# A seventh pair of row tiles in seven block products, with the last pair's sums in the place of x^T

## The chip, the cores and the metric

The kernel runs on one core of one Trainium2 chip. The metric is the device time of one execution in microseconds; three executions of the kernel before were timed, and one more was profiled. Engines are named as in the profile: PE (TensorE, matrix products), DVE (VectorE), ACT (ScalarE), POOL (GpSimd), SP (SyncE, which issues the loads).

## The reference

Two layers of an encoder over 256 tokens of width 1024, each a half-step feed-forward, a mixer of two groups of attention heads, and another half-step feed-forward, every one followed by a layer norm. The change touches the feed-forward blocks, of which there are four:

```python
def swiglu(x, w_in, w_out):
    h = x @ w_in
    gate, up = h[..., :D_FF], h[..., D_FF:]
    return (jax.nn.silu(gate) * up) @ w_out
...
    x = layer_norm(ALPHA * x + 0.5 * swiglu(x, ffn1_w_in[l], ffn1_w_out[l]), ln_g[l, 0], ln_b[l, 0])
```

With `D_FF` = 2816, the hidden activation g has 22 column tiles of 128, and `w_out` has 22 row tiles of 128 x 1024. The product g @ `w_out` is called the second product here, x @ `w_in` the first.

## The kernel before

All products are made in fp32 precision from two fp32r halves: a value is split into a high half (`wh` of a weight, made by a copy on ACT) and a low half (`wl`, made on DVE as value minus high half, L73 and L119), and each product is the sum of three matmuls: high by high, high by low, low by high. All weights are loaded from memory once, as row tiles of 128 x 1024 (512 KB), into five buffers named `raw`; the halves have nine buffers each.

A feed-forward block goes as follows. The first four column tiles (`first`) and then the other 18 (`col`, in twos) of g are computed transposed, so that g has its columns on the partitions: for each column tile 16 wide matmuls of 512 columns (L419) with x^T, high and low half side by side in the tile `xx`, and 16 narrow ones of 256 columns (L424). `xx` holds x^T as 8 blocks of (half, token tile, 128). DVE and ACT then apply SiLU, multiply and split g.

Then comes the second product, whose result has four blocks: two tiles of 128 tokens by two halves of 512 columns. There are two ways to add a row tile of `w_out` to it. A *single* (`step`, L503) takes 12 matmuls of 512 columns for one row tile: 3 parts, 2 token tiles, 2 halves. A *pair* (`pair`, L527) takes two row tiles together as a 2 x 2 block product in seven products instead of eight (Winograd's form of Strassen's scheme): 21 matmuls for two row tiles. Four of the seven products gather in PSUM tiles `pp` over all pairs and are combined at the end (L540 to L549); three go straight to the accumulators `acc`. For a pair, `_make_pair` (L76 and on) loads both row tiles (`a` and `b`) and makes four combinations of their blocks on DVE (L86 to L89: into `t`, into a half of `a`, and into `t4`, whose halves are the tiles ending in `f`), and then the halves of `b`, `t`, `a` and `f` (L73; three tiles of 1024 columns and one of 512). On the other side, `sums` (L448 on) makes four combinations of the pair's blocks of g: four steps of 128 columns on DVE into `sf`, a copy of 512 on ACT (L461) for the high halves, and a difference of 512 on DVE (L462) for the low ones. The sums stay until their pair is used. Those of the first three pairs lie in buffers of `xp`, beside the residual x; those of the next three lie in the pool `tp` (tag `tmp`, seven buffers, two for each pair).

The order on PE is written out by hand. `STR` names the pairs of row tiles that go as pairs. The other row tiles are singles; the last seven of them are the *tail*, and `PLAN` gives the order of the rest: `o` is a single and `S` a pair. After the plan the tail runs over the first token tile, then over the second, while the first one's layer norm runs. In before, pairs 3 to 8 (row tiles 6 to 17) are pairs, row tiles 0, 1, 2 are the singles of the plan, and 3, 4, 5, 18 to 21 are the tail. The other engines' orders come from a scheduler, which follows the program's order and priorities; preparing a weight has a low priority, and `W.get` asks for weights up to nine half-buffers ahead (a pair counts as four).

The weights of the first block's plan and tail are numbered 44 on: in before the singles are 44, 45 and 47, the pairs 46 and 48 to 52, the tail 53 to 59; so `wl52a` is the low half of the last pair's `a`.

Of the kernel before, what the change touches and what calls it, by code (L numbers as in the profile page):

```python
# [24 lines left out]
JT = DFF // P  # L25
# [12 lines left out]
NB = 4  # L38
LATER = 100
WARM = 9  # L40
STR = (3, 4, 5, 6, 7, 8)
PLAN = "o o S o S S S S S"

# [90 lines left out]
def encoder_kernel(  # L136
# [36 lines left out]

    singles = [k for k in range(JT) if k // 2 not in STR]
    singles, tail = singles[: len(singles) - TAIL], singles[len(singles) - TAIL :]
    plan, left, pairs = [], list(singles), list(STR)
    for u in PLAN.split():
        plan.append((u, (left if u == "o" else pairs).pop(0)))
# [28 lines left out]
    xx = cp.tile([P, KT, 2, 2, P], F32R, name="xx")  # L207
# [153 lines left out]
    def ffn(l, n, last=False):  # L361
# [42 lines left out]
        def col(*js, flip=False):  # L404
# [26 lines left out]
            for j, hs, tl, ws in ts:  # L431
                for s in range(2):
                    two(hs, ws, s)
                    nc.scalar.copy(tl[:, s], hs[s][:, 1, :])  # L434
                    dv.tensor_tensor(tl[:, s], hs[s][:, 0, :], tl[:, s], ALU.add)  # L435
                nc.scalar.activation(tl[:, 0], tl[:, 0], AF.Silu)  # L436
                gv = tl[:, 1]
                dv.tensor_tensor(gv, tl[:, 0], gv, ALU.mult)  # L438
                q, jj = divmod(j, 2)
                n = P if q in STR and jj == 0 else SEQ  # L440
                nc.scalar.copy(gs[q][:, jj, 0, 0:n], gv[:, 0:n])  # L441
                dv.tensor_tensor(gs[q][:, jj, 1, 0:n], gv[:, 0:n], gs[q][:, jj, 0, 0:n].bitcast(F32), ALU.subtract)
                if q in STR and jj:
                    sums(q, ts[0][2][:, 1], gv)
# [3 lines left out]
        def sums(q, g0, g1):  # L448

            f = tp.tile([P, 4, P], F32, tag="tmp", name=f"sf_{nm}_{q}")  # L450
            if STR.index(q) < 3:
                s = xp.tile([P, 2, 4, P], F32R, tag="x", name=f"s_{nm}_{q}")
                sh, sl = s[:, 0], s[:, 1]
            else:
                sh, sl = (tp.tile([P, 4, P], F32R, tag="tmp", name=f"s{c}_{nm}_{q}") for c in "hl")
            a11, a21, a12, a22 = g0[:, 0:P], g0[:, P:SEQ], g1[:, 0:P], g1[:, P:SEQ]
            dv.tensor_tensor(f[:, 0], a21, a22, ALU.subtract)
            dv.tensor_tensor(f[:, 1], a11, f[:, 0], ALU.subtract)
            dv.tensor_tensor(f[:, 2], a21, a11, ALU.subtract)
            dv.tensor_tensor(f[:, 3], a12, f[:, 1], ALU.subtract)  # L460
            nc.scalar.copy(sh, f)  # L461
            dv.tensor_tensor(sl, f, sh.bitcast(F32), ALU.subtract)  # L462
            sm[q] = sh, sl
# [43 lines left out]
        def pair(q, w, first, final):  # L507
            b11, b21, b22, t4, t1, t2, t3 = w
            if first:
                for c in (5, 7, 1, 6):  # L510
                    pp[c] = ps.tile([P, 512], F32, tag="b", name=f"pp_{nm}_{c}")
            sh, sl = sm[q]
            blk = lambda kk, t: [gs[q][:, kk, e, t * P : (t + 1) * P] for e in range(2)]
            smb = lambda c: (sh[:, c], sl[:, c])
            s1, s2, s3, s4 = (smb(c) for c in range(4))
            for o, (ah, al), (bh, bl) in (
                (acc[0][0][1], blk(1, 0), b21),
                (acc[0][1][1], s4, b22),
                (pp[5], s1, t1),
                (pp[7], s3, t3),  # L520
                (pp[1], blk(0, 0), b11),
                (pp[6], s2, t2),
                (acc[1][0][1], blk(1, 1), t4),
            ):
                own = any(o is p for p in pp.values())
                for e, (g, ww) in enumerate(((ah, bh), (ah, bl), (al, bh))):
                    mm(o, g, ww, start=(own and first and e == 0), stop=(own and final and e == 2))  # L527

        for u, k in plan:
            w = W.get(wi)  # L530
            wi += 1
            if u == "S":
                pair(k, w, k == STR[0], k == STR[-1])
            else:
# [3 lines left out]
        c = 0.5 / ALPHA  # L538
# [24 lines left out]
        for n_, (i, cs) in enumerate(todo):  # L563
# [3 lines left out]
            if last and cs is acc[1] and i == TAIL - SPLIT - 1:  # L567
                s, a = acc[1][1][:2]
# [413 lines left out]
```

## Time and profile before

| | |
|---|---|
| three timed runs | 928.75, 930.30, 930.32 us; median 930.3 |
| the profiled execution | 929.28 us, span 927.5 us |
| granted PE clock, mean | 0.997 |
| PE busy | 99% of the span |
| DVE busy | 87% |
| ACT busy | 62% |
| read from memory | 174.35 MB, 189 GB/s over the span |

The second product with its tail takes some 57 us in each of the four blocks; in the first block it begins at 128 us of the span. In the timeline view a row gives the start in us, the duration in us, the engine, the line, the operation with the tiles written and read, and in brackets the idle time just before with what ended it. Instructions of one engine overlap a little in their pipelines, so what an engine can do is read from start to start, not from the durations.

### The profile page before, as it was taken

To read this page: it belongs to the slowest core of one execution; us is meant where nothing else is said; L and a number is where in the kernel's file an instruction comes from. 1 tells how busy PE (TensorE), PEld (TensorE's weight loads), DVE (VectorE), ACT (ScalarE), POOL (GpSimd) and SP (SyncE) were. 2 spreads that over 40 slices of the span, in tenths; PEclk is the share of its full clock that TensorE was granted. 3 is DMA by queue.
4 is the path that set the end of the run, shared out by engine and by line. 5 is a ranking of instruction groups with operands and counts; after the bars stand their busy time and mean duration, and the time that the engine had idled before them with its cause. 6 is when DMAs were issued, how large, how long until landed. Compare 5 with 4: busy or idle time off the path is not lost.

```text
span 927.5 us, 13795 instructions
## 1 busy us (share of the span) xinstructions
PE 919.1 (99%) x4958; PEld 784.9 (85%) x4958; DVE 804.9 (87%) x1388; ACT 577.8 (62%) x982; POOL 17.0 (2%) x27
## 2 busy tenths in 40 slices
PE   9999999999999999999999999999999999999996
PEld 6888888888878888888888888888888888888885
DVE  7898899998987677899986888999988876888997
ACT  5768656546865666656646666664478656666660
POOL 0000000000000000000000000000000000000000
PEclk9999999999999999999999999999999999999998
DMA  8976445774426755545775665466844365665451
GB/s 320 313 265 203 160 137 191 246 260 154 128 90 206 248 182 182 159 136 191 257 262 196 187 192 168 136 231 208 290 112 137 100 236 188 189 192 163 136 205 46
DMA packets 51380, 176.30 MB, mean 190 GB/s; under 512 B 6512, under 2 KB 8304, under 8 KB 51312
## 3 DMA queue, kind: packets, MB, share of 16 engines
q1 hardware_dynamic: 51024, 175.03, 58.0%
q8 instruction: 39, 0.64, 0.3%
q10 hardware_dynamic: 288, 0.39, 0.1%
q14 instruction: 29, 0.24, 0.1%
HBM read 174.35 MB, written 1.05 MB: 189 GB/s over the span
## 4 chain that ended last, share of the span: by engine, by line
PE 98%; DMA 1%; DVE 1%; SPq 0%; issue 0%; ACT 0%; DVEq 0%
PE hg L419 14%; PE hu L419 14%; PE acc L503 12%; PE hb L381 9%; PE hu L424 7%; PE hg L424 7%; PE pp L527 7%; PE acc L527 5%; PE ao L840 5%; PE os L776 1%; PE pj_sq L617 1%; PE pj_sq L619 1%; PE pj_dv L617 1%; PE pj_sq L618 1%; PE pj_dq L618 1%; PE pj_dv L619 1%
## 5 line engine op out<-in xcount | busy, mean ns | idle before, releaser
L119 DVE TENSOR_TENSOR wl<-raw,wh 128x1024 fp32r<-128x1024 f32 (+1 forms) x271 | 325.2, 1207 | 57.0 <-PE hg L424 20.2
L118 ACT CAST wh<-raw 128x1024 fp32r<-128x1024 f32 (+1 forms) x271 | 282.1, 1046 | 99.7 <-PE acc L503 14.8
L419 PE MATMUL hg<-xx,wh 128*128 128x512 f32 x576 | 143.1, 390 | 0.0
L419 PE MATMUL hu<-xx,wh 128*128 128x512 f32 x576 | 142.3, 389 | 0.0
L419 PEld LDWEIGHTS hu<-xx,wh 128*128 128x128 f32 x576 | 108.1, 188 | 22.5
L419 PEld LDWEIGHTS hg<-xx,wh 128*128 128x128 f32 x576 | 106.6, 188 | 21.2
L503 PE MATMUL acc<-wh,g 128*128 128x512 f32 (+1 forms) x326 | 90.5, 386 | 0.0
L424 PE MATMUL hg<-xx,wl 128*128 128x256 f32 x576 | 81.0, 283 | 0.0
L424 PE MATMUL hu<-xx,wl 128*128 128x256 f32 x576 | 80.9, 283 | 0.0
L424 PEld LDWEIGHTS hg<-xx,wl 128*128 128x128 f32 x576 | 75.4, 191 | 1.6
L424 PEld LDWEIGHTS hu<-xx,wl 128*128 128x128 f32 x576 | 74.3, 192 | 0.0
L503 PEld LDWEIGHTS acc<-wh,g 128*128 128x128 f32 x326 | 60.9, 188 | 12.2
L381 PE MATMUL hb<-wh,xx 128*128 128x512 f32 x256 | 69.5, 391 | 0.4 <-ACT wh L118 0.4
L381 PEld LDWEIGHTS hb<-wh,xx 128*128 128x128 f32 x256 | 47.7, 188 | 11.3 <-ACT wh L118 1.6
L503 PE MATMUL acc<-wl,g 128*128 128x512 f32 (+1 forms) x163 | 51.7, 385 | 0.0
L434 ACT COPY tl<-hg 128x256 f32<-128x256 f32 x72 | 26.7, 371 | 30.9 <-PE hg L419 27.4
L434 ACT COPY tl<-hu 128x256 f32<-128x256 f32 x72 | 26.9, 373 | 19.6 <-PE hu L424 16.8
L381 PE MATMUL hb<-wl,xx 128*128 128x512 f32 x128 | 38.9, 390 | 0.0
L441 ACT CAST g<-tl 128x128 fp32r<-128x128 f32 (+1 forms) x72 | 26.7, 371 | 19.2 <-DVE tl L438 18.2
L840 PE MATMUL ao<-wh,xx 128*128 128x512 f32 x128 | 37.0, 398 | 0.0
L503 PEld LDWEIGHTS acc<-wl,g 128*128 128x128 f32 x163 | 30.6, 188 | 6.1
L436 ACT ACTIVATE tl<-tl 128x256 f32<-128x256 f32 x72 | 30.1, 418 | 6.5 <-DVE tl L435 5.7
(1140 smaller groups left out, 1576.3 us busy)
## 6 DMA issues: line engine op xcount, KB each, us to landing
raw<-in_f_in_dram SPq DMA_DIRECT2D x144, 512.0 KB, 4.4
raw<-in_f_out_dram SPq DMA_DIRECT2D x40, 512.0 KB, 4.5
raw<-in_m_in_dram SPq DMA_DIRECT2D x36, 512.0 KB, 4.4
raw<-in_f_b_dram SPq DMA_DIRECT2D x29, 512.0 KB, 4.3
raw<-in_m_out_dram SPq DMA_DIRECT2D x8, 512.0 KB, 5.0
raw<-in_m_out_dram SPq DMA_DIRECT2D x16, 256.0 KB, 4.4
lng<-in_ln_g_dram SPq DMA_DIRECT2D x6, 512.0 KB, 4.9
lnb<-in_ln_b_dram SPq DMA_DIRECT2D x6, 512.0 KB, 6.2
```

Of the source, the lines that this page charges most:

```text
L118: nc.scalar.copy(wh[:, s], raw[:, s])
L119: nc.vector.tensor_tensor(wl[:, s], raw[:, s], wh[:, s].bitcast(F32), ALU.subtract)
L381: mm(hb[s], xx[:, k, g, t, :], ww[:, 512 * s : 512 * s + 512], start=(k == 0 and e == 0), stop=(k == KT - 1 and e == 2))
L419: mm(hs[s], ws[s][0][:, k * P : (k + 1) * P], xx[:, k], start=(k == 0 and not flip), stop=(k == KT - 1 and flip), skip_group_check=flip)
L424: mm(hs[s][:, 1, :], ws[s][1][:, k * P : (k + 1) * P], xx[:, k, 0], start=(k == 0 and flip), stop=(k == KT - 1 and not flip), skip_group_c ...
L434: nc.scalar.copy(tl[:, s], hs[s][:, 1, :])
L436: nc.scalar.activation(tl[:, 0], tl[:, 0], AF.Silu)
L441: nc.scalar.copy(gs[q][:, jj, 0, 0:n], gv[:, 0:n])
L503: mm(a, g, ww[:, s], start=(k == ka and e == 0), stop=(k == kb and e == 2))
L527: mm(o, g, ww, start=(own and first and e == 0), stop=(own and final and e == 2))
L617: mm(o, xx[:, k, 0, t, :], wh[:, s], start=(k == 0), stop=False)
L840: mm(acc[t][h], xx[:, k, g, t, :], ww[:, s], start=(k == 0 and e == 0), stop=(k == KT - 1 and e == 2))
```

## The change

Pairs 4 to 10 go as pairs, seven in place of six; row tiles 0 to 7 are the singles, 0 in the plan and 1 to 7 in the tail. The plan is one single and then seven pairs in a row. The last pair's sums of g (tiles 20 and 21) get no buffers of their own: their high and low halves are written over the first two blocks of `xx`, x^T, which has been read by then.

```diff
-STR = (3, 4, 5, 6, 7, 8)
-PLAN = "o o S o S S S S S"
+STR = (4, 5, 6, 7, 8, 9, 10)
+PLAN = "o S S S S S S S"
...
             if STR.index(q) < 3:
                 s = xp.tile([P, 2, 4, P], F32R, tag="x", name=f"s_{nm}_{q}")
+                sh, sl = s[:, 0], s[:, 1]
+            elif q == JT // 2 - 1:
+                s = xx[:, 0:2].rearrange("p k e t c -> p k (e t) c")
                 sh, sl = s[:, 0], s[:, 1]
             else:
                 sh, sl = (tp.tile([P, 4, P], F32R, tag="tmp", name=f"s{c}_{nm}_{q}") for c in "hl")
```

Lines after L453 stand three further down in the changed kernel (L457 to L462 are L460 to L465 there, L540 to L549 are L543 to L552). The first block's single of the plan is weight 44, the pairs are 45 to 51, the tail 52 to 58.

The scheduler's order on DVE moves with it, in the same way in all four blocks. The first place is the end of the first products in the first block, behind the last step on column tile 21 (`tl_21`); `sf_10` are the sums of tiles 20 and 21. Before:

```order
L438 TENSOR_TENSOR tl_21_1376<-tl_21_1376 128x256
L73 TENSOR_TENSOR wl48t<-raw48t,wh48t 128x1024
L442 TENSOR_TENSOR g_10_198<-tl_21_1376,g_10_198 128x256
L87 TENSOR_TENSOR raw49t<-raw49a,raw49b 128x512
L73 TENSOR_TENSOR wl48a<-raw48a,wh48a 128x1024
L88 TENSOR_TENSOR raw49a<-raw49b,raw49t 128x512
L73 TENSOR_TENSOR wl48f<-t_48_1496,wh48f 128x512
L89 TENSOR_TENSOR t_49_1547<-raw49b,raw49a 128x512
L73 TENSOR_TENSOR wl49b<-raw49b,wh49b 128x1024
```

And now:

```order
L438 TENSOR_TENSOR tl_21_1370<-tl_21_1370 128x256
L86 TENSOR_TENSOR raw47t<-raw47a 128x512
L442 TENSOR_TENSOR g_10_198<-tl_21_1370,g_10_198 128x256
L460 TENSOR_TENSOR sf_10_1451<-tl_20_1341,tl_21_1370 128x128
L87 TENSOR_TENSOR raw47t<-raw47a,raw47b 128x512
L461 TENSOR_TENSOR sf_10_1451<-tl_20_1341,sf_10_1451 128x128
L88 TENSOR_TENSOR raw47a<-raw47b,raw47t 128x512
L463 TENSOR_TENSOR sf_10_1451<-tl_21_1370,sf_10_1451 128x128
L465 TENSOR_TENSOR xx<-sf_10_1451,xx 128x512
L89 TENSOR_TENSOR t_46_1467<-raw46b,raw46a 128x512
L73 TENSOR_TENSOR wl46f<-t_46_1467,wh46f 128x512
L89 TENSOR_TENSOR t_47_1530<-raw47b,raw47a 128x512
```

At this place DVE now makes the last pair's sums between the combinations of pair 47's weights, writes their low halves into `xx`, and only then makes `t4` of pair 46 and its low half; before, no sums stood here.

The second place is the end of the plan in the first block, from the last pair's `a` on: `wl_` with a number is a low half of a tail weight, `x_in` the residual, `v` and `u` the tiles in which the block products are combined. Before:

```order
L73 TENSOR_TENSOR wl52a<-raw52a,wh52a 128x1024
L73 TENSOR_TENSOR wl52f<-t_52_1700,wh52f 128x512
L119 TENSOR_TENSOR wl_1723<-raw_1721,wh_1722 128x1024
L119 TENSOR_TENSOR wl_1750<-raw_1748,wh_1749 128x1024
L119 TENSOR_TENSOR wl_1756<-raw_1754,wh_1755 128x1024
L119 TENSOR_TENSOR wl_1762<-raw_1760,wh_1761 128x1024
L540 SCALAR_TENSOR_TENSOR x_in_601<-pp_1_1519,x_in_601 128x512
L543 TENSOR_TENSOR v_1793<-pp_6_1520,v_1793 128x512
L119 TENSOR_TENSOR wl_1768<-raw_1766,wh_1767 128x1024
L545 TENSOR_TENSOR u_1797<-pp_5_1517,v_1793 128x512
L119 TENSOR_TENSOR wl_1806<-raw_1804,wh_1805 128x1024
L540 SCALAR_TENSOR_TENSOR x_in_601<-u_1797,x_in_601 128x512
```

And now:

```order
L73 TENSOR_TENSOR wl51a<-raw51a,wh51a 128x1024
L73 TENSOR_TENSOR wl51f<-t_51_1718,wh51f 128x512
L119 TENSOR_TENSOR wl_1741<-raw_1739,wh_1740 128x1024
L119 TENSOR_TENSOR wl_1768<-raw_1766,wh_1767 128x1024
L543 SCALAR_TENSOR_TENSOR x_in_593<-pp_1_1502,x_in_593 128x512
L546 TENSOR_TENSOR v_1811<-pp_6_1503,v_1811 128x512
L119 TENSOR_TENSOR wl_1774<-raw_1772,wh_1773 128x1024
L548 TENSOR_TENSOR u_1815<-pp_5_1500,v_1811 128x512
L119 TENSOR_TENSOR wl_1780<-raw_1778,wh_1779 128x1024
L543 SCALAR_TENSOR_TENSOR x_in_593<-u_1815,x_in_593 128x512
L550 TENSOR_TENSOR v_1811<-pp_7_1501,v_1811 128x512
L119 TENSOR_TENSOR wl_1786<-raw_1784,wh_1785 128x1024
```

Four tail weights stood ahead of the first step of the combination, and now two; the seventh tail weight now has seven steps of the combination ahead of it, where it had five.

## Prediction

> **What bounds the kernel now.** I read the page first, then the waits of PE (TensorE), then DVE (VectorE) and PE in order of time through the second products of the first feed-forward block.
>
> ```profile
> span 927.5 us, 13795 instructions
> PE 919.1 (99%) x4958; PEld 784.9 (85%) x4958; DVE 804.9 (87%) x1388; ACT 577.8 (62%) x982; POOL 17.0 (2%) x27
> PEclk9999999999999999999999999999999999999998
> ```
>
> ```profile
> PE wps L217 <- PEq L971: 0.8, 1, 0.8
> PE hb L381 <- ACT wh L118: 0.4, 1, 0.4
> ```
>
> PE is busy for 919.1 of 927.5 us at the full granted clock, and the two waits shown, 1.2 us together, are all that the waits view has for it, both in the first 11 us. So every matmul that goes is worth its time, and every wait that comes is paid in full. The next engine is DVE, and in the stretch that the change touches it is hardly behind. In this row of the windows view (length, busy us of PE, weight loads, DVE, ACT and POOL, then clock, DMA share and GB/s):
>
> ```profile
> 128.00:165.00 37.00, 37.00 (x165) 30.65 (x164) 36.06 (x44) 23.91 (x29) 0.00 (x0) 1.00 0.56 186
> ```
>
> DVE works 36.06 of 37 us. It makes the weights' low halves (`wl`) and the pairs' four combinations. One pair of the steady run, on DVE in order of time (start, duration), and the last `a` tile of the last pair:
>
> ```profile
> 146.97 0.69 DVE L86 TENSOR_TENSOR raw51t<-raw51a 128x512 f32<-128x512 f32 x1
> 147.57 0.69 DVE L87 TENSOR_TENSOR raw51t<-raw51a,raw51b 128x512 f32<-128x512 f32 x1
> 148.18 1.22 DVE L73 TENSOR_TENSOR wl51b<-raw51b,wh51b 128x1024 fp32r<-128x1024 f32 x1
> 149.31 0.68 DVE L88 TENSOR_TENSOR raw51a<-raw51b,raw51t 128x512 f32<-128x512 f32 x1
> 149.91 1.22 DVE L73 TENSOR_TENSOR wl51t<-raw51t,wh51t 128x1024 fp32r<-128x1024 f32 x1
> 151.05 0.68 DVE L89 TENSOR_TENSOR t<-raw51b,raw51a 128x512 f32<-128x512 f32 x1
> 151.65 1.22 DVE L73 TENSOR_TENSOR wl51a<-raw51a,wh51a 128x1024 fp32r<-128x1024 f32 x1
> 152.79 0.68 DVE L73 TENSOR_TENSOR wl51f<-t,wh51f 128x512 fp32r<-128x512 f32 x1
> 153.39 0.68 DVE L86 TENSOR_TENSOR raw52t<-raw52a 128x512 f32<-128x512 f32 x1
> ...
> 158.07 1.22 DVE L73 TENSOR_TENSOR wl52a<-raw52a,wh52a 128x1024 fp32r<-128x1024 f32 x1
> ```
>
> From 146.97 to 153.39 a pair takes DVE 6.42 us with no gap: five steps of 512 columns that follow each other by 0.60 and three of 1024 by 1.135 (5 x 0.60 + 3 x 1.135 = 6.41). PE over the last pair (first matmul; the first that reads `wl52a`; then the tail, with the first and the seventh `wl`):
>
> ```profile
> 160.04 0.39 PE L527 MATMUL acc<-wh52b,g 128*128 128x512 f32 x1
> ...
> 162.99 0.39 PE L527 MATMUL pp<-wl52a,g 128*128 128x512 f32 x1
> ...
> 164.80 0.61 PE L503 MATMUL acc<-wh,g 128*128 128x512 f32 x2
> 165.25 0.62 PE L503 MATMUL acc<-wl,g 128*128 128x512 f32 x2
> ...
> 173.41 0.62 PE L503 MATMUL acc<-wl,g 128*128 128x512 f32 x2
> ```
>
> 160.04 to 164.80 is 4.76 us for 21 matmuls, 0.2267 us each. So PE eats a pair in 4.76 us and DVE makes one in 6.41: within a run of pairs PE gains 1.65 us per pair on DVE. It gets away with it today because DVE starts early: `wl52a` is ready at 158.07 + 1.22 = 159.29 and read at 162.99, a slack of 3.70 us. The other blocks stand the same:
>
> ```profile
> L73 DVE TENSOR_TENSOR wl138a<-raw138a,wh138a x1: 1212/1212/1212, 436.3 to 436.3; 128x1024 fp32r<-128x1024 f32 x1
> L527 PE MATMUL pp<-wl138a,g x1: 389/389/389, 441.2 to 441.2; 128*128 128x512 f32 x1
> L73 DVE TENSOR_TENSOR wl284a<-raw284a,wh284a x1: 1217/1217/1217, 894.3 to 894.3; 128x1024 fp32r<-128x1024 f32 x1
> L527 PE MATMUL pp<-wl284a,g x1: 389/389/389, 899.2 to 899.2; 128*128 128x512 f32 x1
> ```
>
> Here too 4.9 us lie between the two starts, as in the first block (158.07 and 162.99).
>
> **The change part by part.** *Removed on PE.* Two row tiles as singles cost 24 matmuls, as a pair 21: three fewer in each of four blocks, 12 x 0.2267 = 2.72 us. That is all there is to gain.
>
> *Added on DVE ahead of the last pair.* The rows of other kinds that the count needs (steps of 128, then of 256; the brackets give DVE's idle time and its releaser):
>
> ```profile
> 97.07 0.29 DVE L459 TENSOR_TENSOR sf<-tl 128x128 f32<-128x128 f32 x1
> 97.27 0.28 DVE L457 TENSOR_TENSOR sf<-tl,tl 128x128 f32<-128x128 f32 x1
> 97.48 1.22 DVE L119 TENSOR_TENSOR wl<-raw,wh 128x1024 fp32r<-128x1024 f32 x1
> ...
> 101.26 0.69 DVE L462 TENSOR_TENSOR sl<-sf,sh 128x512 fp32r<-128x512 f32 x1 [0.69 <-ACT sh L461]
> ...
> 113.12 0.69 DVE L462 TENSOR_TENSOR sl<-sf,sh 128x512 fp32r<-128x512 f32 x1 [1.13 <-ACT sh L461]
> ...
> 118.06 0.41 DVE L435 TENSOR_TENSOR tl<-hu,tl 128x256 f32<-128x256 f32 x1
> 118.39 0.41 DVE L442 TENSOR_TENSOR g<-tl,g 128x256 fp32r<-128x256 f32 x1
> ```
>
> Small steps follow by 0.20 (128 columns) and 0.33 (256). I count in DVE's order from `sl` of the pair of tiles 16 and 17 (113.12) to the start of the last pair's `a`. Before: 19 steps of 1024, 26 of 512, 16 of 256 = 42.5 us (158.07 - 113.72 = 44.35 measured, so 1.8 us of it is waiting). After: 20, 33, 14, and 10 of 128 (two pairs' sums, which before were made earlier in the block) = 49.2 us. That is 6.67 us more (1.135 + 7 x 0.60 - 2 x 0.335 + 10 x 0.20). The start of the stretch stays put, because DVE waits there in both: the rows at 101.26 and 113.12 show it waiting for ACT's copy of the sums, behind work that PE releases.
>
> *Extra waits.* Ahead of the last `a`, DVE now waits for ACT's copy of the new sums (0.69, the row at 101.26) and then takes `wl46f` directly behind the step that makes its input, so it waits for ACT again (0.7, by the same kind of copy). At most 1.4, at least 0 if the 1.8 us of waiting shrink by as much; I take 0.7, the middle, since only part of that waiting is of this kind. Queued behind both waits on DVE is every later pair; PE waits for those.
>
> *When PE wants it.* Two singles fewer (2 x 2.72) and one pair more (4.76) ahead of it: 0.68 earlier, at 162.31. DVE has it at 159.29 + 6.67 + 0.7 = 166.66. PE thus waits **4.35 us** over the run of pairs (3.65 to 5.05). It begins at the fifth pair: taken back by 1.65 per pair from 4.35, the waits have added up to 2.70 at the sixth and 1.05 at the fifth, and the fourth still lies 0.6 ahead of PE.
>
> *The tail.* The seven tail weights were made ahead of the tail, with the block products' combination put in between. The seventh in before:
>
> ```profile
> 170.99 1.21 DVE L119 TENSOR_TENSOR wl<-raw,wh 128x1024 fp32r<-128x1024 f32 x1
> ```
>
> 170.99 + 1.21 = 172.20, read at 173.41: 1.2 us of slack. After, from the last `a` to the seventh tail `wl`, DVE has 8 steps of 1024 and 8 of 512 up to the end of it (12.75 us between the two starts, by 1.135 + 0.60 + 6 x 1.135 + 7 x 0.60), and PE 8 matmuls, six tail tiles at 1.36 and 0.45: 10.42. Coming from a pair that PE waited for, it waits **2.33 us** more. A wait for a transfer can add to this, as one did in before:
>
> ```profile
> 167.56 1.05 ACT L118 CAST wh<-raw 128x1024 fp32r<-128x1024 f32 x1 [2.36 <-DMA raw<-in_f_out_dram]
> ```
>
> In before the stretch took 12.92 instead of the counted 11.54, so 2.33 to 3.7; I take 2.4, the low end, because DVE runs later against the loads than it did.
>
> *What follows.* The other half of the tail (9.5 us of PE) needs no new weight; the layer norm has one step of 512 less and one of 1024 more ahead of it, 0.5 us, against a start that is 0.5 us earlier behind the accumulators' end. I cost it at nothing; were that cover gone, it costs 0.5 per block. What DVE owes is paid by PE's waiting, so the next stage starts with the old lead.
>
> *The sums in the place of x^T.* They are made from the last column tiles' results, so the matmuls that read x^T last are done before there is anything to write: no wait. The transposed rows return there only after the tail's first half, which stands behind the last pair on PE. *ACT* gets the high halves of the same tiles to copy and is busy 23.91 of 37. *DMA*: the same bytes, two loads of a pair for two single ones on SP's queue, which the added pair moves past nothing else; in the steady run above DVE never waited for a load. POOL has nothing. All these at nothing; if a pair's load were late by its whole slack, it would show as a DVE wait for ACT or DMA, at most the 2.36 us of the row above.
>
> *Restart of PE* after a wait, bounded by the length of a weight load that may have to come first (the 188 ns of this group):
>
> ```profile
> L503 PEld LDWEIGHTS acc<-wh,g 128*128 128x128 f32 x326 | 60.9, 188 | 12.2
> ```
>
> 0 to 0.19, 0.1 taken.
>
> **Sum per block**: 4.35 + 2.4 + 0.1 - 0.68 = 6.2 us, four times 24.7. The profiled run took 929.28 (span 927.5 and 1.8 around it): 954.0. The median of the three runs, 930.3, lies 1.0 above it, so I forecast **955.0 us**.
>
> [...]
>
> **Rivals.**
> *The lead holds (faster).* If DVE still had every pair ahead of PE, only the 12 matmuls would count: 930.3 - 2.7 = 927.6. It decides at 3.70 - 0.68 = 3.0 us of extra work ahead of the last pair, and the tail asks for more. For it: the lead of 3.70 us, and 1.8 us of waiting that DVE could fill. Against: 6.67 - 1.8 is still 4.9. Chance 0.04.
> *Change without effect.* DVE is 1 us better per pair than counted, so that waits and saving cancel: 929 to 932. Nothing in the rows speaks for it; 0.01.
> *Pairs wait, the tail recovers.* If PE's waiting lets DVE refill during the last pair, the 2.4 goes: 3.8 per block, 945.5. Against it: DVE's order puts the combination between the weights, and it has no idle time to refill. 0.07.
> *The clock drops as well.* The opening matmuls show the slow clock:
>
> ```profile
> 0.77 3.92 PE L217 MATMUL wps<-const-bfloat16-1.0 128*128 128x512 bf16 x9 [0.77 <-PEq L971]
> ```
>
> 3.92 / 9 = 0.436 us each. At that pace a pair takes PE 9.15 us, and three pairs and half a tail would lose some 14 us more per block (3 x 2.74 and 42 x 0.436 against 11.9 with the waits): 1011. The page's clock line shows no drop, but also no waits to cause one. [...] 0.02.
>
> **How the numbers follow.** Forecast 0.86: per block from 3.65 + 2.33 - 0.68 = 5.3 (951.5) to 5.05 + 3.7 + 0.2 - 0.68 = 8.3 (963.4). The range reaches down to the recovering tail: 945 to 963. A measurement of this kernel tells about 0.2% (1.9 us) from no change. Faster 0.04, same 0.01, slower 0.95 (forecast, recovering tail and clock).
>
> **What would show it.** Right: PE's waits, now 1.2 us, grow to some 27, nearly all on DVE's `wl`; PE's pairs start 4.76 us apart up to the fourth and about 6.4 from the fifth; DVE shows no gap between the sums of tiles 20 and 21 and the last tail weight; the waits look alike in all four blocks; the first products and the mixer keep their lengths. Wrong: PE waits stay under 3 us (the lead held), or none stand in the tail, or they are put down to DMA, or the granted clock falls in the second products, or the mixer starts to wait.

## The result, and the profile after

The changed kernel takes 960.39 us (median of four runs, 960.15 to 960.92) against 930.24 us before: a ratio of 1.0329, 95% interval 1.0311 to 1.0347. The forecast was 955.0 in a range of 945 to 963. One of the four executions of the run with two singles put back, further down, took 5273.77 us, far from its other three (958.53 to 960.18), and is left out. The profiled execution took 960.48 us, span 958.7. From the page of the kernel after:

```profile
span 958.7 us, 13813 instructions
PE 934.9 (98%) x4946; PEld 778.2 (81%) x4946; DVE 826.1 (86%) x1432; ACT 582.9 (61%) x993; POOL 17.0 (2%) x27
PEclk9999999999999999999999999999999999999999
PE 75%; DVE 20%; issue 4%; ACT 1%; DVEq 0%
```

Twelve matmuls fewer on PE, as planned, the clock line as before, and yet PE's busy time is 15.8 us longer. The last row is the head of the chain of work that ended last: a fifth of it lies on DVE, where in before it was 1%. The waits of PE in the kernel after:

```profile
PE tr_y L327 <- DVE x L355: 2.9, 3, 1.0
PE acc L506 <- DVE wl L119: 2.7, 4, 0.7
...
PE acc L530 <- DVE wl49b L73: 0.6, 1, 0.6
```

Apart from the opening one (as in before) all are for DVE, and three pairs in each block wait. But twelve rows of 0.6, 2.7 and 2.9 make some 13 us, and the kernel lost 30. The rest is not in this view: a wait that a weight load sits out ahead of the matmul is listed with the weight loads, and one that is shorter than a matmul shows only as a gap. PE over the third to the last pair of the first block, in order of time:

```profile
140.10 0.39 PE L530 MATMUL acc<-wh47b,g 128*128 128x512 f32 x1
...
144.87 0.39 PE L530 MATMUL acc<-wh48b,g 128*128 128x512 f32 x1
...
147.60 0.39 PE L530 MATMUL pp<-wh48a,g 128*128 128x512 f32 x1
148.05 0.50 PE L530 MATMUL pp<-wl48a,g 128*128 128x512 f32 x1
...
150.00 0.39 PE L530 MATMUL acc<-wh49b,g 128*128 128x512 f32 x1
151.00 0.50 PE L530 MATMUL acc<-wl49b,g 128*128 128x512 f32 x1 [0.61 <-DVE wl49b L73]
...
156.42 0.39 PE L530 MATMUL acc<-wh50b,g 128*128 128x512 f32 x1
...
162.83 0.39 PE L530 MATMUL acc<-wh51b,g 128*128 128x512 f32 x1
...
167.30 0.50 PE L530 MATMUL pp<-wl51a,g 128*128 128x512 f32 x1
...
169.25 0.62 PE L506 MATMUL acc<-wh,g 128*128 128x512 f32 x2
```

Pair to pair it is 4.77, 5.13, 6.42 and 6.41 us. The first late weight is `wl48a` in the fourth pair (0.45 between two starts where 0.23 is the pace, with no bracket); from the fifth pair on PE runs at DVE's 6.41. The lost time is best read from stage to stage: from the stage's first matmul to its tail 41.39 us (127.86 to 169.25) where before it was 36.72, though PE has 0.68 less to do.

DVE over the same time in the kernel after: the two waits for ACT, the last `a`, the seventh tail weight, and the first layer norm's last step:

```profile
113.26 0.69 DVE L465 TENSOR_TENSOR sl<-sf,sh 128x512 fp32r<-128x512 f32 x1 [1.63 <-ACT sh L464]
...
134.65 0.69 DVE L465 TENSOR_TENSOR xx<-sf,xx 128x512 fp32r<-128x512 f32 x1 [0.69 <-ACT xx L464]
...
136.76 0.69 DVE L73 TENSOR_TENSOR wl46f<-t,wh46f 128x512 fp32r<-128x512 f32 x1 [0.69 <-ACT wh46f L72]
...
166.04 1.21 DVE L73 TENSOR_TENSOR wl51a<-raw51a,wh51a 128x1024 fp32r<-128x1024 f32 x1
...
178.84 1.21 DVE L119 TENSOR_TENSOR wl<-raw,wh 128x1024 fp32r<-128x1024 f32 x1
...
189.45 0.74 DVE L355 SCALAR_TENSOR_TENSOR x<-x,rs,lnb 128x512 f32<-128x512 f32 x1
```

And the tail on PE, from the seventh `wl` to the mixer's first matmul:

```profile
180.11 0.73 PE L506 MATMUL acc<-wl,g 128*128 128x512 f32 x2
...
188.64 0.65 PE L327 MATMUL tr_y<-ident,x 128*128 128x128 f32 x4
190.25 0.66 PE L327 MATMUL tr_y<-ident,x 128*128 128x128 f32 x4 [0.96 <-DVE x L355]
...
192.81 0.39 PE L620 MATMUL pj_dq<-wh,xx 128*128 128x512 f32 x1
```

From `wl51a` read (167.30) to the seventh tail `wl` read is 12.81 us for work of 10.42. Then PE waits 0.96 for the layer norm's last step before it can transpose: that wait was not there before. The whole second product of the first block takes 64.95 us (127.86 to 192.81), before 57.11; the four blocks are longer by 7.84, 8.27, 8.24 and 7.09, 31.4 in all. First products, column tiles and mixer agree with before to 0.1 us (the mixer: 97.58 in both).

### The profile page after: what moved, and what is told of

Read it like the earlier page. It is cut to its first block, busy times and chain, and to the rows that moved or that the text cites. A ratio compares the mean times of both kernels' runs of the same rounds, so it can differ in the third digit from the quotient of the medians.

```text
span 958.7 us, 13813 instructions
## 1 busy us (share of the span) xinstructions
PE 934.9 (98%) x4946; PEld 778.2 (81%) x4946; DVE 826.1 (86%) x1432; ACT 582.9 (61%) x993; POOL 17.0 (2%) x27
## 4 chain that ended last, share of the span: by engine, by line
PE 75%; DVE 20%; issue 4%; ACT 1%; DVEq 0%
PE hg L419 13%; PE hu L419 13%; PE hb L381 9%; PE hu L424 7%; PE hg L424 7%; PE ao L843 5%; PE acc L506 4%; DVE t L89 2%; PE os L779 1%; PE pj_sq L620 1%; PE pj_sq L622 1%; PE pj_dv L620 1%; PE pj_dv L622 1%; PE pj_sq L621 1%; PE pj_dq L621 1%
## 5 line engine op out<-in xcount | busy, mean ns | idle before, releaser
L119 DVE TENSOR_TENSOR wl<-raw,wh 128x1024 fp32r<-128x1024 f32 (+1 forms) x263 | 315.6, 1206 | 58.7 <-PE hg L424 22.3
L118 ACT CAST wh<-raw 128x1024 fp32r<-128x1024 f32 (+1 forms) x263 | 273.6, 1046 | 97.7 <-PE acc L506 10.5
L506 PE MATMUL acc<-wh,g 128*128 128x512 f32 (+1 forms) x262 | 73.2, 387 | 0.0
L506 PEld LDWEIGHTS acc<-wh,g 128*128 128x128 f32 x262 | 48.9, 188 | 10.2
L506 PE MATMUL acc<-wl,g 128*128 128x512 f32 (+1 forms) x131 | 44.2, 402 | 3.6 <-DVE wl L119 2.7
L435 DVE TENSOR_TENSOR tl<-hg,tl 128x256 f32<-128x256 f32 x72 | 30.1, 418 | 8.5 <-ACT tl L434 8.5
L506 PEld LDWEIGHTS acc<-wl,g 128*128 128x128 f32 x131 | 23.1, 188 | 15.4 <-DVE wl L119 12.1
```

The costliest lines, as they stand in the source:

```text
L118: nc.scalar.copy(wh[:, s], raw[:, s])
L119: nc.vector.tensor_tensor(wl[:, s], raw[:, s], wh[:, s].bitcast(F32), ALU.subtract)
L506: mm(a, g, ww[:, s], start=(k == ka and e == 0), stop=(k == kb and e == 2))
```

## The experiments

The theory under test, "DVE-late": DVE cannot make the pairs' weights at PE's pace, and the change spends the lead that hid this. The rivals: the new place of the sums costs something; the loads or the five raw buffers of an added pair do; the row of seven pairs without singles between does; DVE's order alone is to blame. "Before" is 929.6 to 929.9 in the experiments.

### Six pairs, with the change's two other parts

```diff
-STR = (4, 5, 6, 7, 8, 9, 10)
-PLAN = "o S S S S S S S"
+STR = (5, 6, 7, 8, 9, 10)
+PLAN = "o o S o S S S S S"
```

> Pairs 5 to 10 with six pairs, the plan of the kernel before and the last pair's sums in the place of x^T: the place alone, without the seventh pair. DVE-late theory (DVE makes a pair slower than PE eats it, so each microsecond of DVE work ahead of the last pair beyond the lead of before is waited for): DVE has 45.05 us of counted work from the sums of tiles 16 and 17 to the last pair's a tile, against 42.5 before and 49.2 with seven pairs, so the lead of 3.7 us shrinks to 0 to 1.2 and PE does not wait in the run of pairs; in the tail up to 1.1, at the layer norm up to 0.8: 931 to 938 us. Rival (the place of the sums costs, by writes that wait for readers of x^T or the other way round): about as slow as the changed kernel, 955 to 962.

Measured: 940.76 us, ratio 1.0114 (1.0099 to 1.0129), 2.8 us above DVE-late's range and far under the rival's 955. PE's waits in this run:

```profile
PE pj_dk L621 <- DVE rs L348: 2.7, 2, 1.3
PE acc L506 <- DVE wl L119: 1.8, 4, 0.7
PE pj_dk L621 <- DVE wl L119: 1.7, 2, 0.8
PE hb L381 <- DVE wl L119: 1.1, 2, 0.9
```

No pair waits, so the sums' place in `xx` costs nothing in the run of pairs. What is left stands in the tail and at the start of the next stage (`pj_dk`, the mixer; `hb`, the next first product), and is for DVE again. I read it so, without a run that takes it apart: with the last row tiles as pairs, DVE makes sums and pair weights later, and PE pays for it after the stage. I had let the lateness end with the stage; it does not (both mixers are 2.8 us longer than before).

### One DVE step less per pair, seven pairs and six

```diff
-            dv.tensor_tensor(t4, r1[:, a], r0[:, b], ALU.subtract)
...
-            (t4,) = self._halves(i, t4, "f")
+            (t4,) = self._halves(i, r1[:, a], "f")
```

In the changed kernel:

> The changed kernel without the step that makes t4 (the fourth combination of a pair's weights; the second row tile's left half is used raw, so one of the seven products is another one): loads, buffers, PE's instructions and the order of the pairs stay, 0.60 us of DVE per pair goes. DVE-late: 7 x 0.60 fewer ahead of the last a tile and the wait for ACT ahead of wl46f gone, so of the 5.2 us of waiting in the run of pairs 0.3 to 0.5 is left; tail (2.4) and layer norm (0.8) stay: 940 to 944 us. Rival (PE waits because the pairs' loads or buffers come late, or by the order of the pairs): no change, 959 to 961.

Measured: 938.08 us, ratio 1.0087 (1.0070 to 1.0103), 22.3 us under the changed kernel and some 2 us below the expected range. 28 steps of 0.60 are 16.8 us; in this trace DVE's two waits for ACT of 0.69 (at 134.65 and 136.76 above) are gone too, and in four blocks those are 5.5. No pair waits any more: from the stage's first matmul to its tail it is 36.04 us (128.26 to 164.30), 5.35 less than in the changed kernel. The tail and the layer norm still wait:

```profile
PE acc L504 <- DVE wl L117: 3.0, 5, 0.7
PE tr_y L325 <- DVE x L353: 2.9, 3, 1.0
```

The same edit in the kernel before:

> The kernel before (six pairs), without the fourth combination: the last of a pair's weights is cut from the raw tile, so DVE has one step of 512 columns less per pair (the output is not the reference's). The same edit brought the changed kernel 22 us. DVE-late: in the kernel before PE never waits for DVE, so there is nothing to get back: 929 to 931. If DVE's steps cost PE time in some other way than by waits (both at the same memory): 4 x 6 x a part of 0.6 us, 920 to 927.

Measured: 929.85 us, ratio 1.0001 (0.9991 to 1.0011). The same steps are worth 22 us to the one kernel and nothing to the other: a DVE step costs these kernels only where PE waits for it.

### Two DVE steps less per pair

```diff
-            dv.tensor_tensor(r0[:, b], r1[:, b], ta[:, a], ALU.add)
-            dv.tensor_tensor(t4, r1[:, a], r0[:, b], ALU.subtract)
```

> The changed kernel without two of the five steps of 512 columns that DVE does for each pair: the fourth combination is replaced by the raw tile, and the step that adds the third combination to the raw tile is left out (both change what is computed, so the output is not the reference's). PE's work is that of the changed kernel. If DVE's lateness is the whole cost: DVE reaches the last pair's `a` 14 x 0.60 = 8.4 us earlier than in the changed kernel, some 3 us ahead of PE, which about covers the tail; the 2.7 us of matmuls saved are seen, less 0 to 0.9 us per block at the tail and the layer norm: 927.5 to 931 us. If part of the loss is something else (loads of the added pair, buffers, the place in x^T): it stays where one step less left it, 936 to 939.

Measured: 928.92 us, ratio 0.9988 (0.9979 to 0.9998). PE's only wait in this run but for the opening one:

```profile
PE tr_y L324 <- DVE x L352: 1.9, 2, 0.9
```

With DVE quick enough the seventh pair shows its saving, less the 1.9 us of the layer norm in two blocks. In the last block, which has no such wait, the second product takes 62.53 us to the end of the span against 63.19 before: 0.66 of the 0.68 that three matmuls make. So the pairs' loads, the five raw buffers and the sums' place cost nothing that can be seen. Without `t4` its buffer in `tmp` is free as well, in this run and the last; but the step left out here in addition frees no buffer, and it is worth 9.2 us (938.08 to 928.92). The price of the change is DVE's time, and all that it could gain is 2.7 us.

### More DVE work with six pairs in the old order

```diff
-            dv.tensor_tensor(ta[:, a], r0[:, b], r0[:, a], ALU.subtract)
+            for _ in range(3):
+                dv.tensor_tensor(ta[:, a], r0[:, b], r0[:, a], ALU.subtract)
```

> The kernel before (six pairs, eight singles ahead and in the tail as they were, sums in their old places), but each pair's first combination is computed three times over, which changes no result and adds two DVE steps of 512 columns per pair. If DVE's lateness is the whole cause: ten of the twelve steps lie between the last column tiles and the last pair's `a`, 10 x 0.60 = 6.0 us against a slack of 3.7, so PE waits 2.3 to 3.7 us in the run of pairs, 2.4 to 2.9 in the tail as soon as the lead is gone, 0 to 0.5 at the layer norm: 4.7 to 7 per block, 949 to 957 us in all, with pairs that end up about 7.6 us apart on DVE. If it takes a seventh pair, the new place of the sums or the new order of row tiles to bring the waits: 929 to 932, no change.

Measured: 950.66 us, ratio 1.0220 (1.0204 to 1.0235), as DVE-late has it: nothing of the change is in this kernel but more work on DVE. The pairs on DVE are 7.86 us apart (starts of `wl50a` and `wl51a`, 147.81 and 155.67). Only the sixth pair waits on PE, then the tail; 2.9 of the 21 us stand in the two mixers, so lateness was carried on here too:

```profile
PE pj_dk L619 <- DVE wl L120: 1.3, 2, 0.7
PE pp L528 <- DVE wl284t L73: 1.0, 1, 1.0
```

### The tail's weights first

Their copies and differences get a higher priority than the pairs' in the changed kernel.

```diff
-            with self.tc.high_priority(0 if i < 3 else -LATER):
+            with self.tc.high_priority(URGENT if i in self.urgent else 0 if i < 3 else -LATER):
```

> The changed kernel with a higher priority for the seven tail weights, so that four of the eight steps that combine the block products move behind the seventh tail weight on DVE (10.35 us counted from the last a tile to it, where 12.75 were; PE needs 10.42). DVE-late: the waits in the run of pairs stay at 5.2 us per block, those of the tail fall from 2.4 to under 0.3, the one at the layer norm shrinks or stays: 948 to 952 us. Rival (the tail waits for its loads): the waits move to ACT and DMA and the time stays within 2 us of the changed kernel's 960.

Measured: 970.05 us, ratio 1.0435 (1.0419 to 1.0450): wrong by the sign. The second products are 2.6 to 3.2 us shorter than in the changed kernel in each of the first three blocks and the wait at `tr_y` is gone, but the mixers are 8.1 and 8.9 us longer:

```profile
PE pj_dk L628 <- DVE wl L120: 10.2, 2, 5.1
PE hb L388 <- DVE wl L120: 2.0, 1, 2.0
```

The new order does not make DVE's work less. What it put off met PE in the next stage, in one piece of 5.1 us each, and that was dearer than many short ones (see the last section). It is not a load that PE waits for there: by the order on the two engines ACT had the high half of that weight ready at 184.98, and DVE came to the low half at 197.70.

### Two singles put back between the pairs

```diff
-TAIL = 7
+TAIL = 5
...
-PLAN = "o S S S S S S S"
+PLAN = "o S o S o S S S S S"
```

> The changed kernel with two of the seven tail singles put back ahead, one behind the first pair and one behind the second (three singles between the first pairs, five in the tail). PE's matmuls are the same in number. Each single ahead gives DVE 2.72 - 1.14 = 1.6 us, so the run of pairs waits 5.2 - 3.2 = 2.0 us; but the tail's first half is 2.7 us shorter for PE and 2.3 for DVE, so its wait grows by 0.4, and the layer norm has 2.7 us less cover, so its wait grows from 1.0 to 3.7. DVE-late, with DVE's sum of work deciding: 8 to 8.5 us of waits per block as now, 956 to 964 us. If the row of seven pairs without singles between them is the cause: the 3.2 us per block are gained, 945 to 951.

Measured: 959.35 us, ratio 1.0313 (1.0296 to 1.0331), 0.1% from the changed kernel's time. In the run of pairs and at the layer norm the waits are where the expectation put them: the pairs start 4.76 us apart up to the last but one, and the last two fall behind (5.01 to the last one, which waits 0.6 in the view of PE's waits alone), 1.9 us in all where 2.0 were expected; the layer norm's wait has grown from 1.0 to 3.4 (3.7 expected):

```profile
PE tr_y L327 <- DVE x L355: 10.3, 3, 3.4
...
PE acc L530 <- DVE wl53b L73: 0.6, 1, 0.6
```

The tail's first half waits 1.6 us (171.29 to 179.72 for 6.80 of work), where 2.8 were expected. So the three come to 7.0 us in the first block, against 8.7 in the changed kernel (5.35, 2.37 and 0.96), and that the total is the same is luck. Behind the long wait PE's matmuls go at half their pace for a while:

```profile
188.06 1.32 PE L327 MATMUL tr_y<-ident,x 128*128 128x128 f32 x8 [3.42 <-DVE x L355]
...
190.53 0.63 PE L506 MATMUL acc<-wl,g 128*128 128x512 f32 x1
190.95 1.05 PE L506 MATMUL acc<-wh,g 128*128 128x512 f32 x2
```

From 189.68 to 193.09 us their starts are 0.43 apart, where 0.23 is the pace; the granted clock is 0.51 from 189.6 to 193.1, and in the first three blocks PE works at half clock for 3.4, 5.6 and 3.4 us, which costs half of that, 6.2 us. By this estimate the kernel without the slow clock would take some 953 us, below what DVE-late had (956 to 964) and above what the rival had (945 to 951). So the row of seven pairs is not the main cause, but neither does the sum of the waits stay: singles between the pairs take some 7 of the 30 us off, and the slow clock gives them back.

### The transposes of the layer norm later

```diff
-TCUT = 3
+TCUT = 1
```

> The changed kernel with the transposes of the first half's layer norm (tr_y) two half singles (1.4 us of PE) later, ahead of the last half single of the tail instead of the third from last. It tests the term that the prediction put at nothing: tr_y's second four wait 1.0 us for DVE's last layer-norm step in three of four blocks. If that wait is all of it, it goes: 957 to 958.5 us. If the late DVE only moves it on, into the next stage's first matmuls, which then wait for the rows of x^T: 959.5 to 962.

Measured: 963.73 us, ratio 1.0361 (1.0344 to 1.0379), worse than either. The wait at `tr_y` is gone and the second product is 0.3 to 0.4 us shorter in the first two blocks, but 0.4 longer in the third, and both mixers are 1.5 longer:

```profile
PE pj_dq L620 <- ACT xx L331: 2.2, 2, 1.4
PE pj_dk L621 <- DVE wl L119: 1.4, 2, 0.7
```

The next stage's first matmuls read the rows that are transposed here. So the 0.96 cannot be taken out by this move: it is DVE's lateness, and of the two places tried the old one is the cheaper.

### Two of the combinations on GpSimd

An attempt at a better kernel: seven pairs, with DVE relieved by an engine that has nothing to do.

```diff
-            dv.tensor_tensor(ta[:, a], r0[:, b], r0[:, a], ALU.subtract)
-            dv.tensor_tensor(ta[:, b], r0[:, b], r1[:, b], ALU.add)
+            nc.gpsimd.tensor_tensor(ta[:, a], r0[:, b], r0[:, a], ALU.subtract)
+            nc.gpsimd.tensor_tensor(ta[:, b], r0[:, b], r1[:, b], ALU.add)
```

> The changed kernel with two of a pair's four combinations (the two that fill ta) on POOL in place of DVE: 12 steps of 0.60 fewer on DVE ahead of the last a tile. DVE-late: if DVE's own steps keep their length, PE's waits in the run of pairs vanish, the tail keeps 0.3 and the layer norm 0.8 per block: 929 to 934 us. If POOL's reads slow DVE's steps while it runs, or a POOL step takes over 2 us, part or all of it is lost: 935 to 960, and DVE's steps of 1024 columns grow beyond 1.22 us. A rival without DVE in it (loads, buffers) expects 959 to 961.

Measured: 985.70 us, ratio 1.0599 (1.0583 to 1.0615), out of both ranges. DVE and then GpSimd in this run, in order of time:

```profile
156.67 1.21 DVE L73 TENSOR_TENSOR wl49t<-raw49t,wh49t 128x1024 fp32r<-128x1024 f32 x1
157.80 2.31 DVE L73 TENSOR_TENSOR wl49a<-raw49a,wh49a 128x1024 fp32r<-128x1024 f32 x1
160.03 1.78 DVE L73 TENSOR_TENSOR wl49f<-t,wh49f 128x512 fp32r<-128x512 f32 x1
```

```profile
156.97 2.06 POOL L86 TENSOR_TENSOR raw50t<-raw50a 128x512 f32<-128x512 f32 x1 [3.12 <-DVE t L89]
158.99 2.27 POOL L87 TENSOR_TENSOR raw50t<-raw50a,raw50b 128x512 f32<-128x512 f32 x1
```

The two take turns. GpSimd's first step is there at 156.97 but ends 1.15 us behind the end of `wl49t` (157.88); `wl49a` starts at 157.80 and ends 1.08 behind the end of that step (159.03); GpSimd's second ends 1.14 behind `wl49a`; `wl49f` 0.56 behind that. Read from the ends, the steps of the two follow each other and do not overlap. So a step of 0.60 on DVE is replaced by one of 1.1 for which DVE has to stand still, and a pair takes DVE 7.4 us (`wl49a` at 157.80, `wl50a` at 165.21) instead of 6.4, which is what two such exchanges make (6.4 - 2 x 0.60 + 2 x 1.1). To see whether the turns or the chain over two engines does it, GpSimd gets work beside the kernel before that nobody waits for:

```diff
+            scr = self.tmp.tile([P, 96], F32, tag="scr", name=f"scr{i}", bufs=1)
+            for _ in range(8):
+                nc.gpsimd.tensor_tensor(scr, r0[:, 0:96], r0[:, 96:192], ALU.subtract)
```

> The kernel before, and GpSimd does eight steps of 96 columns per pair beside it, which subtract two pieces of the pair's first raw tile into a tile that nobody reads: DVE's and PE's work is the same and nothing waits for GpSimd's results. If GpSimd and DVE take turns, each step holding the other off (in the run with two combinations on GpSimd, a step of 512 held DVE off by some 1.1 us): 8 x 0.2 to 0.4 us per pair, 8 to 16 us by the last pair's `a` against a slack of 3.7, and 2.4 in the tail: 955 to 990 us, with DVE steps of 1024 columns longer than 1.22 us wherever GpSimd is busy. If only the chain of steps over two engines made that run slow: 929 to 932, all DVE steps at 1.22.

Measured: 953.87 us, ratio 1.0255 (1.0240 to 1.0270), just under the range. DVE in this run, beside GpSimd and, in the last two rows, behind its last step:

```profile
157.37 1.41 DVE L73 TENSOR_TENSOR wl51a<-raw51a,wh51a 128x1024 fp32r<-128x1024 f32 x1
158.71 0.87 DVE L73 TENSOR_TENSOR wl51f<-t,wh51f 128x512 fp32r<-128x512 f32 x1
...
163.03 1.21 DVE L73 TENSOR_TENSOR wl52t<-raw52t,wh52t 128x1024 fp32r<-128x1024 f32 x1
164.16 0.68 DVE L92 TENSOR_TENSOR t<-raw52b,raw52a 128x512 f32<-128x512 f32 x1
```

From 146.69 to 161.10 us every DVE step is 0.2 us longer beside GpSimd, whether it has 512 columns (0.87 to 0.88 against 0.68) or 1024 (1.41 against 1.21): one small GpSimd step per DVE step (eight of GpSimd's in 7.92 us from 153.50, eight of DVE's in 8.00 from 153.10). The turns cost DVE the time, then; eight steps a pair cost 1.6 us, the low end of what I took. The two traces put the time at 1.1 us for a GpSimd step of 512 columns and 0.2 for one of 96.

## Why the prediction was right, and where it was short

The mechanism was right: PE gains on DVE in a run of pairs, the lead of 3.7 us is spent, and the difference is paid as waits, in the run of pairs and in the tail, alike in all four blocks. Pairs 4.8 apart and then 6.4 from the fifth, the unchanged column tiles and mixer, the unchanged clock: as said. The sum was 24.7 us and 31.4 came. By its terms, in the first block:

- **Run of pairs**, 4.35 forecast: 5.2 measured (`wl51a` read at 167.30; unstalled, PE would have read it at 162.09). DVE had it at 167.25, not 166.66. The count of steps (49.2) holds: from 113.86, where DVE goes on from the row at 113.26, to 166.04 are 52.18 us, so 2.99 of waiting, 1.2 more than the 1.83 of before. The step that failed is the middle I took between 0 and 1.4 for DVE's extra waits: both waits of 0.69 that I had named came, in the places named, and the old waiting shrank by only 0.2. DVE also got its start 0.14 later, and PE reached the stage 0.2 earlier.
- **Tail**, 2.4: measured 2.37 (169.25 to 181.14, 11.89 us; before 9.52). No wait for a load was added; the low end was the right end.
- **Layer norm**, nothing: measured 0.8 (the tail's second half to the mixer 11.67, before 10.87), nearly all the 0.96 at `tr_y`, and 1.2 in the second and third block; the last block has no such transposes. The step that failed is "What DVE owes is paid by PE's waiting, so the next stage starts with the old lead". PE's waiting pays up to the weight it waited for and leaves no lead behind it: PE reads the seventh tail weight at 180.11, 0.06 us after DVE has it (178.84 + 1.21), where before it was 1.2 us after. From there PE, at full pace, is at the first transposes in 8.5 us and through them in 9.2, and DVE ends the norm's last step after 10.1 (189.45 + 0.74). The 0.5 was miscounted as well: between the seventh weight and that step DVE's order in the two traces has one step of 512 fewer, as I said, but three of 1024 in both, and the way is 0.2 us shorter (10.61 us from start to start, before 10.84). And there was no cover to count on in the first block: before, the norm's last step ended at 182.57, and the second four transposes began at 182.63. The transposes' experiment shows that the term is real at both places tried.
- **Restart**, 0.1: 0.15 (the run of pairs lost 5.35, the wait 5.2). It shows as a first matmul of 0.50 instead of 0.39, 0.33 to the next start instead of 0.23.
- **Saving**, 0.68 per block: the two-step experiment shows 0.66.

Together 0.9 too little in the run of pairs of each block, and 0.8 to 1.2 at the layer norm of the first three: the 6.7 us that were missing. That the range held it is partly luck: its upper end had the 1.4, which came, and a tail of 3.7, which did not, and the layer norm, which it had at nothing, took up that room. Two of my signs were misjudged. PE's waits were to "grow to some 27" in the waits view, and they grew to 13; the rest stands in weight loads' waits, gaps and stretched matmuls. And that DVE shows no gap behind the sums of tiles 20 and 21 contradicted my own sum: the wait at 136.76 is one that it had counted. The rivals fell: the lead did not hold, the tail did not recover. The sums in the place of x^T, the loads and the five raw buffers were costed at nothing, and the two-step experiment bears that out. Buffers of their own for the last sums weren't tried. That the second and third block lost more than the first (8.27 and 8.24 against 7.84) lies in the kernel before: the run of pairs takes 41.39 us in all four blocks now, and the whole second product 64.9 in the first three, but before it took 57.11 in the first and 56.68 in the next two, because there the first block's transposes were already a little late.

## What to carry to other kernels

When the bound engine is 99% busy and the next one 87%, look for the stretch where the second is the slower of the two and ask how much lead it has there: an edit that takes work from the first and gives some to the second is then priced by the second (here 2.7 us of PE's work were saved, and the kernel lost 30 us waiting for DVE). Count the feeder's steps from its last fixed point to the late weight, add in full each wait that you can name, and follow the lateness until it has been paid, into the tail, the norm and the next stage: changing the order moved the wait three times here and never made the kernel more than 1.0 us faster, once because behind waits of 3.4 us the granted clock fell to 0.51, which ate what had been gained. And try what an idle engine costs the busy one before handing it work: here each of GpSimd's steps of 512 columns made DVE stand still for 1.1 us.

## What the runs showed of the hardware

*GpSimd and VectorE take turns* in these two runs, on the steps with two inputs that they have there: 1.1 us of standing still for DVE per 512-column GpSimd step, nearly twice the DVE step of 0.60 that it replaced, and 0.2 us per step of 96 columns.

*The clock.* The waits of the changed kernel (1.2 us at most) left the granted clock at 0.998. In two experiments single waits were longer than 3 us. The tail weights first, PE at the mixer's start and the windows view (length, busy us of PE, weight loads, DVE, ACT, POOL, then the clock):

```profile
198.97 0.79 PE L628 MATMUL pj_dk<-wl,xx 128*128 128x512 f32 x1 [5.12 <-DVE wl L120]
199.56 0.63 PE L629 MATMUL pj_dk<-wh,xx 128*128 128x512 f32 x1
...
202.97 0.47 PE L628 MATMUL pj_dq<-wl,xx 128*128 128x512 f32 x1
203.28 0.40 PE L629 MATMUL pj_dq<-wh,xx 128*128 128x512 f32 x1
```

```profile
190.00:194.00 4.00, 3.48 (x15) 2.21 (x13) 4.00 (x7) 0.00 (x0) 0.00 (x0) 1.00 0.22 45
199.00:201.00 2.00, 2.00 (x5) 1.61 (x6) 2.00 (x2) 1.18 (x2) 0.00 (x0) 0.50 0.99 209
```

After 5.1 us without work the matmuls follow each other by 0.43 instead of 0.23, at half the clock, for 4 us: some 2 us more on top of the wait. After the 3.4 us at `tr_y` in the run with singles between the pairs it is the same (0.43 apart from 190.53 to 192.66), and both runs have a mean clock of 0.99. So the drop in clock to which the prediction gave 0.02 is measured in this case, with single waits of 3.4 and 5.1 us, though not in the changed kernel. The opening matmuls, from which the prediction took the pace of its slow clock (0.436 us each), do not show it by themselves: the windows view of before has a granted clock of 1.00 over them (0.77 to 4.69 us). The 0.43 at 0.50 to 0.51 bears the pace out. Two shorter waits, of 1.9 us in the run with combinations on GpSimd and of 2.0 us at `hb` in the one with the tail weights first, left the clock at 1.00 (the second by the run's mean of 0.991, which the two waits of 5.1 us account for); between 2.0 and 3.4 us no run has one in the view of PE's waits. So in these kernels many short waits are cheaper than one long one of the same sum.
